# Nineteen TensorE steps of a list-scheduled kernel get later places, with what depends on them

## The chip, the cores and the metric

The kernel runs on one core of a Trainium2 chip. That core has five engines with queues of their own: TensorE (PE), VectorE (DVE), ScalarE (ACT), GpSimd (POOL) and SyncE (SP), which mostly issues transfers. The metric is the time of one execution on the device in microseconds (us), as the median of several runs.

## The reference

One layer of a streaming encoder: `x` is 1024 tokens by 1024 features, float32.

```python
mod = silu(c) @ ada_w + ada_b                      # six vectors of 1024: shift, scale, gate, twice
h = modulate(rms_norm(x, mix_norm_w), sh_m, sc_m)
proj = h @ w_in                                    # one input projection for both head groups
y_r = rwkv7_group(proj[..., :RWKV_COLS], ...)      # 8 heads x 64
y_m = mlstm_group(proj[..., RWKV_COLS:], ...)      # 4 heads, qk 64, v 128
x = x + gate * (concat(y_r, y_m) @ w_out)
x = x + gate * hier_moe(modulate(rms_norm(x, ffn_norm_w), sh_f, sc_f), ...)   # 32 experts, 2 per token
out = rms_norm(x, final_norm_w)
```

The RWKV-7 group carries one 64x64 state per head over the tokens:

```python
def step(state, inp):
    r_t, w_t, k_t, v_t, kk_t, b_t = inp
    sa = einsum('bhij,bhj->bhi', state, -kk_t)
    state = state * w_t[:, :, None, :] + sa[..., None] * b_t[:, :, None, :] + v_t[..., None] * k_t[:, :, None, :]
    return state, einsum('bhij,bhj->bhi', state, r_t)
```

The mLSTM group does the same with a matrix memory, gates and a running maximum, in chunks of 64 tokens.

## The kernel before, in words

The kernel computes the RWKV recurrence in chunks of 64 tokens. Eight units are worked off (four pairs of heads, two halves of the sequence), each with eight chunks. A unit has stages, and each is a generator that yields between pieces of work. `unit_prep` makes `AR`, `BK`, `kk`, `Ei` and the products `tp<-AR,BK`, masked by VectorE into `G`. `unit_solve` inverts the triangular matrices that couple tokens within a chunk: it stores `G`, loads it as `N16` (`N` in the profile), and VectorE runs fifteen pairs of `Xt<-N,XD` (a product) and `XD<-Xt` (a sum). The result goes to memory as `img` and comes back as two tiles, `D16` first and then `X16` (`D` and `X` in the profile, issued by SyncE one after the other). `unit_levels` builds larger blocks of the inverse: `tp<-D,G`, VectorE's `T`, `tp<-T,X`, VectorE's `D`, and two more levels. `unit_scan` goes through the chunks: `pr<-st,AR`, VectorE's `R`, `pu<-R,X`, VectorE's copies `UV`, `pp<-UV,BKT`, VectorE's new state `st`, and `py` with the output. `unit_post` normalizes it to `Y`.

Beside the units run the input projection (`lane` steps: three matmuls, since each operand is split into a high and a low part: `hTh,whi`, `hTl,whi`, `hTh,wlo`), the modulation vectors (`ada_w` is multiplied into `ada_rest` on VectorE; TensorE then sums over partitions with `tp<-ones,ada_rest`, and VectorE copies the sums to `modc`), the gates of the mLSTM (`lg`, `row_lf`, `row_m`), its chunks, and transposes of `x` (`lxs`, `lxt`, stored as `xTd`).

The order of this mixer stage is planned. `Recorder.add` doesn't issue an instruction, it records an operation with its dependences; matmuls in a row into the same output tile become one operation, called a step here. `Recorder.flush` then runs a list scheduler over all recorded operations of the five engines, with a cost for each from `Recorder.cost`, ranks by kind of work, and limits by the buffers of each pool. It gives each operation a beginning in planned time (`o.begin`) and appends it to `self.plan`. In the end it issues them in this order:

```python
        for o in self.plan:
            o.run()
```

Each engine executes its own instructions in the order of issue. What an instruction must wait for on other engines, and for a buffer's earlier users, is found when it is issued; so an engine waits at the head of its queue, whatever stands behind. All recorded operations carry line 262 in the profile, the call in `add`. TensorE's steps are numbered in the order of the plan, from 0; there are 1064 of them. The recorded stage takes TensorE from 63.8 to some 800 us of the span. Before it lie the first normalization and modulation, behind it the output projection, the routing and the experts; these are not reordered.

Of the kernel before, what the change touches and what calls it, by code (L numbers as in the profile page):

```python
# [192 lines left out]
PRIO = dict(prep=2, rest=3, lev=1, scan=0, post=4, gates=6, ada=9, rx=8, h=3, chunk=5, split=5, prod=7, fin=4, fetch=5, y=4)  # L193
PE_SLACK = 0.5
RANK = 20.0


class Recorder:
# [55 lines left out]
    def add(self, engine, what, a, kw):  # L254
# [53 lines left out]
        if o.pe:  # L308
            self.last = o

    def flush(self):

        ops = self.ops
# [11 lines left out]
        for o in ops:  # L325
            o.rank = RANK * o.rank - o.bl
        order = {}
# [44 lines left out]
        while left:  # L372
            busy = False
            for e in free:
# [9 lines left out]
                o = best  # L384
# [29 lines left out]
            assert nxt, ('stuck', now, left, [(e, [(o.what, o.seq, [t.key[1] for t in o.tiles]) for o in c[:6]]) for e, c in cand.items()])  # L414
            now = min(nxt)
        self.mode = 'direct'
        for o in self.plan:
            o.run()
        self.ops, self.history, self.last, self.last_pool = [], {}, None, None
# [2130 lines left out]
```

## Time and profile before

| | |
|---|---|
| median of 3 runs | 1297.64 us (1297.11, 1297.64, 1306.84) |
| the profiled execution | 1305.22 us, span 1303.3 us |
| mean granted clock of TensorE | 0.91 of full speed |
| TensorE (PE) busy | 1148.8 us, 88% of the span |
| VectorE (DVE) | 936.3 us, 72% |
| ScalarE (ACT) | 529.2 us, 41% |
| GpSimd (POOL) | 393.9 us, 30% |

The shares are means over stages with different limits, so the trace is read by stretch and by place. A row of the timeline gives the start and the duration in us, the engine, the line, the operation with its output and inputs, and behind it, in brackets, how long the engine was idle before it and what released it. [...]

### The profile page before, as it was taken

The numbers are of one execution on the slowest core, as the hardware profiler recorded it, in microseconds if no ns is written. First come the engines' busy times: TensorE is split into PE (matmuls) and PEld (weight loads), VectorE is DVE, ScalarE is ACT, GpSimd is POOL, SyncE is SP. The second block draws the span as 40 slices with busy tenths as digits, with TensorE's granted clock in tenths as the row PEclk, the third lists the DMA queues.
The fourth block names the chain that finished last, engine by engine and source line by source line (L and its number), as shares of the span: only waits on it lengthen the run. The fifth ranks groups of instructions, "written<-read, shape, count | busy, mean of one in ns | idle before, by whom it ended". The sixth has DMA issues, their size and how long they took to land.

```text
span 1303.3 us, 21771 instructions
## 1 busy us (share of the span) xinstructions
PE 1148.8 (88%) x7807; PEld 836.3 (64%) x7807; DVE 936.3 (72%) x2024; ACT 529.2 (41%) x1021; POOL 393.9 (30%) x464
## 2 busy tenths in 40 slices
PE   3886889797999999999898899995899999898893
PEld 3665666676676777776666677774666666565553
DVE  6699676876656878877748554834688888777766
ACT  5343112142433443333422333644455655455444
POOL 4623134221233242432133323543222222222112
PEclk8887677698999999999899699997799999999997
DMA  9525555475433443322433554699599999999974
GB/s 313 153 69 155 180 174 153 122 204 158 136 96 97 107 112 80 104 69 61 94 119 102 154 159 134 195 361 326 190 306 314 302 289 285 282 320 326 324 264 164
DMA packets 251935, 246.16 MB, mean 189 GB/s; under 512 B 55064, under 2 KB 190362, under 8 KB 251824
## 3 DMA queue, kind: packets, MB, share of 16 engines
q1 hardware_dynamic: 243504, 228.43, 56.2%
q0 software_dynamic: 8320, 16.31, 5.4%
q8 instruction: 62, 1.02, 0.3%
q14 instruction: 49, 0.40, 0.1%
HBM read 212.13 MB, written 44.74 MB: 197 GB/s over the span
## 4 chain that ended last, share of the span: by engine, by line
PE 62%; DMA 16%; DVE 13%; issue 3%; ACT 2%; SPq 1%; POOL 1%; DVEq 0%; ACTq 0%; POOLq 0%
PE lane L262 20%; PE tp L262 14%; PE yd L2049 8%; DMA wd<-in_moe_w_down_dram 4%; PE lane L787 4%; PE lane L788 4%; PE lane L789 3%; DMA ada_w<-in_ada_w_dram 2%; DMA D<-img 2%; DMA wa<-in_moe_w_gate_dram 2%; PE tp L2002 2%; PE lane L189 2%; PE py L262 1%; DMA X<-img 1%; DVE Xt L262 1%
## 5 line engine op out<-in xcount | busy, mean ns | idle before, releaser
L262 PE MATMUL lane<-hTh,whi 128*128 128x512 f32 (+1 forms) x469 | 213.5, 455 | 2.5 <-DVE v L262 0.7
L262 PE MATMUL lane<-hTl,whi 128*128 128x512 f32 (+1 forms) x469 | 192.3, 410 | 5.7 <-DVE hTl L262 5.7
L262 PE MATMUL lane<-hTh,wlo 128*128 128x512 f32 (+1 forms) x469 | 190.8, 407 | 3.1 <-DVE wlo L262 3.1
L262 ACT CAST whi<-wraw 128x512 fp32r<-128x512 f32 (+1 forms) x120 | 71.6, 607 | 163.8 <-PE lane L262 133.8
L2049 PE MATMUL yd<-wd,a 128*112 128x512 f32 x256 | 119.8, 607 | 12.5 <-DMA wd<-in_moe_w_down_dram 9.3
L262 POOL TENSOR_TENSOR wlo<-wraw,whi 128x512 fp32r<-128x512 f32 (+1 forms) x60 | 81.9, 1367 | 97.2 <-ACT whi L262 95.1
L262 PEld LDWEIGHTS lane<-hTh,whi 128*128 128x128 f32 (+1 forms) x469 | 91.0, 194 | 30.9 <-issue 2.2
L262 PEld LDWEIGHTS lane<-hTh,wlo 128*128 128x128 f32 (+1 forms) x469 | 90.9, 194 | 27.2 <-DVE wlo L262 4.8
L262 PEld LDWEIGHTS lane<-hTl,whi 128*128 128x128 f32 (+1 forms) x469 | 91.4, 195 | 20.6 <-DVE hTl L262 8.3
L1972 DVE TENSOR_TENSOR wl<-wa,wh 128x1024 fp32r<-128x1024 f32 x62 | 75.6, 1225 | 40.2 <-ACT wh L1971 38.8
L787 PE MATMUL lane<-wh,xh 128*112 128x512 f32 x256 | 103.9, 406 | 0.0
L788 PE MATMUL lane<-wl,xh 128*112 128x512 f32 x256 | 101.7, 397 | 0.0
L789 PE MATMUL lane<-wh,xl 128*112 128x512 f32 x256 | 100.7, 393 | 0.0
L262 POOL TENSOR_SCALAR sW<-st,WT 128x64 f32<-128x64 f32 x56 | 33.1, 592 | 215.5 <-DVE st L262 129.9
L2076 POOL DMA_INDIRECT x2d<-ys,idx x30 | 44.9, 1496 | 147.4 <-DVE ys L2060 138.5
L2049 PEld LDWEIGHTS yd<-wd,a 128*112 128x112 f32 x256 | 43.5, 182 | 65.4 <-issue 44.6
L1972 DVE TENSOR_TENSOR wl<-wb,wh 128x1024 fp32r<-128x1024 f32 x62 | 76.4, 1233 | 11.3 <-ACT wh L1971 9.6
L1971 ACT CAST wh<-wa 128x1024 fp32r<-128x1024 f32 x62 | 64.8, 1049 | 45.4 <-PE lane L789 36.5
L1971 ACT CAST wh<-wb 128x1024 fp32r<-128x1024 f32 x63 | 66.2, 1051 | 17.4 <-PE lane L789 8.3
L1978 POOL DMA_INDIRECT xt<-xad,idx x32 | 35.0, 1093 | 113.3 <-PE tp L2002 94.9
L262 DVE COPY UV<-pu 64x64 f32<-64x64 f32 x128 | 28.1, 220 | 38.3 <-PE pu L262 36.9
L789 PEld LDWEIGHTS lane<-wh,xl 128*112 128x112 f32 x256 | 44.9, 175 | 14.8 <-DVE xl L2015 0.4
(515 smaller groups left out, 2539.2 us busy)
## 6 DMA issues: line engine op xcount, KB each, us to landing
wd<-in_moe_w_down_dram SPq DMA_DIRECT2D x64, 512.0 KB
wraw<-in_w_in_dram SPq DMA_DIRECT2D x104, 256.0 KB
ada_w<-in_ada_w_dram SPq DMA_DIRECT2D x32, 512.0 KB
wa<-in_moe_w_gate_dram SPq DMA_DIRECT2D x32, 512.0 KB
wa<-in_moe_w_up_dram SPq DMA_DIRECT2D x32, 512.0 KB
wb<-in_moe_w_gate_dram SPq DMA_DIRECT2D x32, 512.0 KB
wb<-in_moe_w_up_dram SPq DMA_DIRECT2D x32, 512.0 KB
ada_w<-in_ada_w_dram SPq DMA_DIRECT2D x32, 256.0 KB
```

The costliest lines, as they stand in the source:

```text
L189: return getattr(eng, what)(*[real(x) for x in a], **{k: real(x) for k, x in kw.items()})
L262: call = lambda: getattr(fn, what)(*[real(x) for x in a], **{k: real(x) for k, x in kw.items()})
L787: nc.tensor.matmul(ps, l[0], r[0], start=first, stop=False)
L788: nc.tensor.matmul(ps, l[0], r[1], start=False, stop=False)
L789: self.mark = nc.tensor.matmul(ps, l[1], r[0], start=False, stop=last)
L1971: nc.scalar.copy(h, src)
L1972: (engs[n] if engs else nc.vector).tensor_tensor(l, src, h.bitcast(F32), op=ALU.subtract)
L1978: return self.nc.gpsimd.indirect_dma_start(out=self.xts[e % 3], out_offset=None, in_=self.xad[:], in_offset=bass.IndirectOffsetOnAxis(ap=s ...
L2002: self.nc.tensor.transpose(pt[:, j, :], v[:, j // 2, j % 2], self.ident[0:SL, 0:SL])
L2049: self.nc.tensor.matmul(y[:, b], a[:, i], d[:, i, b * 512:b * 512 + 512], start=(i == 0), stop=(i == 1))
L2076: self.nc.gpsimd.indirect_dma_start(out=self.x2d[:], out_offset=bass.IndirectOffsetOnAxis(ap=oi, axis=0), in_=ys, in_offset=None, bounds_c ...
```

## The change

A table gives, for nineteen of TensorE's steps, a number of microseconds. A new function `put_off` runs once, between the planning and the issue. It keeps each operation's planned beginning as its key; a step in the table gets its beginning plus the table's number, and whatever depends on it, or takes over a buffer that a postponed operation used before, gets at least the same key. Then the plan is sorted by key; ties keep their order. No operation is added, removed or changed.

```diff
+LATE = {4: 3.4, 44: 2.1, 64: 4.7, 66: 4.9, 73: 3.7, 103: 2.6, 105: 1.5, 107: 1.0, 142: 1.8, 188: 2.1, 196: 3.5, 273: 5.8, 276: 0.9, 358: 0.9, 670: 1.7, 798: 4.5, 911: 1.6, 912: 4.0, 943: 3.0}
...
+    def put_off(self):
+
+        pos = {o: i for i, o in enumerate(self.plan)}
+        old = {}
+        for ts in self.slots.values():
+            for a, b in zip(ts, ts[ts[0].bufs:]):
+                if b.ops_of:
+                    old.setdefault(min(b.ops_of, key=pos.get), []).extend(a.ops_of)
+        key, no = {}, 0
+        for o in self.plan:
+            key[o] = max([o.begin] + [key[d] for d in o.deps if key[d] > d.begin] + [key[d] for d in old.get(o, ()) if d is not o and key[d] > d.begin])
+            if o.pe:
+                key[o] = max(key[o], o.begin + LATE.get(no, 0.0))
+                no += 1
+        self.plan.sort(key=lambda o: (key[o], pos[o]))
+
...
         self.mode = 'direct'
+        self.put_off()
         for o in self.plan:
             o.run()
```

The numbers in the table are the idle times that the trace of the kernel before has ahead of these steps, rounded; they add up to 53.7 us. The order changes at 64 places of TensorE's queue, 45 of VectorE's and 8 of ScalarE's; GpSimd and SyncE keep theirs. The steps, by place (letters are used below):

| place | step | what it is | now behind |
|---|---|---|---|
| A | 4 | `py<-st,AR` | 5 (`lane`), 6 (`tp<-ident,nrm`), 7 (`lane`) |
| B | 44 | twelve gate transposes `lg`, `row_lf`, `row_m` | 45, 46 (`lane`) |
| C | 64 | `tp<-ident,BK` | 65 (the same) |
| D | 66 | `tp<-AR,BK` | 67, 68, 70, 71 |
| E | 73 | `tp<-ones,ada_rest` | 74 (`tp<-D,G`), 75 (`lane`) |
| F | 103, 105, 107 | `pp<-UV,BKT`, `pr<-st,AR`, `tp<-headsel,sq` | 104; 106; none |
| G | 142 | `tp<-D,G` with D16 | 143 (`tp<-ones,ada_rest`) |
| H | 188, 196 | `tp<-ones,ada_rest`, `tp<-ident,lxs` | 189, 190 (`pp`, `py`); 197, 198, 199, 201 |
| I | 273, 276 | `tp<-D,G` with D16, `tp<-AR,BK` | 274, 275, 277, 278; 277, 278 |
| J | 358 | `tp<-D,G` with D16 | 359 (`py`), 360 (`lane`) |
| K | 670 | `tp<-D,G` with D16 | 671 (`pu`), 672 (`lane`), 673 (`tp<-ident,mnv`) |
| L | 798 | `tp<-D,G` with D16 | 799 (`lane`), 800 (gate transposes), 803 (`lane`) |
| M | 911, 912 | `tp<-ident,Y`, `tp<-ident,mnv` | 913 (`tp<-mqo`); 913, 914, 916 |
| N | 943 | `tp<-D,G` with D16 | 944 (`tp<-ident,ex`), 945 to 948 (`lane`) |

At place E, on VectorE's queue, the row sums' copy to `modc` stood ahead of `carry` and `u`, which VectorE takes out of the `lane` step. Before:

```order
L262 SCALAR_TENSOR_TENSOR qko<-lane,phalf,qko 128x510
L262 COPY modc<-tp 128x8
L262 SCALAR_TENSOR_TENSOR qko<-lane,phalf,qko 128x509
L262 TENSOR_SCALAR carry<-lane,pcol 128x1
L262 COPY u_257<-lane 128x3
L262 SCALAR_TENSOR_TENSOR qko<-qks,qko 128x512
L262 TENSOR_TENSOR Xt<-N_1383,XD 64x1
```

and with the change:

```order
L263 SCALAR_TENSOR_TENSOR qko<-lane,phalf,qko 128x510
L263 SCALAR_TENSOR_TENSOR qko<-lane,phalf,qko 128x509
L263 TENSOR_SCALAR carry<-lane,pcol 128x1
L263 COPY u_257<-lane 128x3
L263 COPY modc<-tp 128x8
L263 SCALAR_TENSOR_TENSOR qko<-qks,qko 128x512
L263 TENSOR_TENSOR Xt<-N_1374,XD 64x1
```

`modc` moved behind `u`; the last `qko` product and the first `Xt` of a solve stand directly behind it.

At place F, on VectorE's queue, is the state update `st` of a scan (the numbers behind `N` name buffers). Before:

```order
L262 TENSOR_TENSOR Xt<-N_1383,XD 64x11x11
L262 SCALAR_TENSOR_TENSOR st<-pp,WT,sW 128x64
L262 TENSOR_REDUCE XD<-Xt 64x11
L262 SCALAR_TENSOR_TENSOR k<-lane,pcol,k 128x511
L262 TENSOR_TENSOR Xt<-N_1383,XD 64x12x12
L262 SCALAR_TENSOR_TENSOR cs<-cmask,sw 128x512
```

and with the change:

```order
L263 TENSOR_TENSOR Xt<-N_1374,XD 64x11x11
L263 TENSOR_REDUCE XD<-Xt 64x11
L263 SCALAR_TENSOR_TENSOR k<-lane,pcol,k 128x511
L263 TENSOR_TENSOR Xt<-N_1374,XD 64x12x12
L263 SCALAR_TENSOR_TENSOR cs<-cmask,sw 128x512
L263 SCALAR_TENSOR_TENSOR st<-pp,WT,sW 128x64
```

`st` moved behind four instructions, the scan `cs` among them.

At place L, on TensorE's queue, 798 is the group of 32x32 products with `D_6794` (alternating with two buffers of `G`). Before:

```order
L262 MATMUL tp<-D_6794,G_6398 32x32 x2
L262 MATMUL lane<-hTh,whi 128x512
L262 MATMUL lane<-hTl,whi 128x512
L262 MATMUL lane<-hTh,wlo 128x512
L262 MATMUL tp<-ident,lg_6610 128x4 x4
L262 MATMUL tp<-ident,row_lf 128x4 x4
L262 MATMUL tp<-ident,row_m 128x4 x4
L262 MATMUL tp<-T_6872,X_6802 32x32 x32
L262 MATMUL tp<-ident,vcm 128x128 x4
```

and with the change:

```order
L263 MATMUL tp<-ident,lg_6610 128x4 x4
L263 MATMUL tp<-ident,row_lf 128x4 x4
L263 MATMUL tp<-ident,row_m 128x4 x4
L263 MATMUL lane<-hTh,whi 128x512
L263 MATMUL lane<-hTl,whi 128x512
L263 MATMUL lane<-hTh,wlo 128x512
L263 MATMUL tp<-D_6794,G_6379 32x32 x2
...
L263 MATMUL tp<-T_6921,X_6802 32x32 x32
L263 MATMUL tp<-ident,vcm 128x128 x4
```

One `lane` step (799) now stands ahead of the gate transposes and another (803) behind them, and the D group follows, directly ahead of `tp<-T,X` (801). On VectorE, `T` moved behind three operations on `Y` and a `wlo`.

## Rows read from the trace of the kernel before

**Rows 1.** Two stretches: us, engines' busy us (instructions), PEclk, DMA share, GB/s

```profile
64.00:160.00 96.00, 75.58 (x599) 56.72 (x598) 81.68 (x160) 31.58 (x57) 23.96 (x26) 0.79 0.47 132
800.00:1303.00 503.00, 445.03 (x1982) 309.65 (x1980) 368.78 (x548) 255.89 (x446) 140.88 (x130) 0.94 0.85 278
```

**Rows 2.** Waits of TensorE, 64 to 800 us: total us, times, longest

```profile
PE tp L262 <- DMA D<-img: 17.6, 6, 5.8
```

**Rows 3.** Timeline at place B: start, us, engine, operation, [idle before, releaser]

```profile
105.83 0.76 PE L262 MATMUL lane<-hTh,whi 128*128 128x512 f32 x1 [0.17 <-DVE carry L262]
```

**Rows 4.** Timeline at place E, TensorE

```profile
143.10 3.54 PE L262 MATMUL tp<-ones,ada_rest 128*128 128x1 f32 x16 [3.73 <-issue]
...
149.26 0.96 PE L262 MATMUL tp<-X,T 32*32 32x32 f32 x28
```

**Rows 5.** Timeline at place E, VectorE

```profile
146.68 0.17 DVE L262 COPY modc<-tp 128x8 f32<-128x8 f32 x1 [0.71 <-PE tp L262]
...
147.42 0.21 DVE L262 TENSOR_SCALAR carry<-lane,pcol 128x1 f32<-128x1 f32 x1
...
149.73 0.15 DVE L262 TENSOR_TENSOR Xt<-N,XD 64x1 f32<-64x1 f32 x1
```

**Rows 6.** Timeline at place F, VectorE and TensorE

```profile
170.53 0.28 DVE L262 SCALAR_TENSOR_TENSOR st<-pp,WT,sW 128x64 f32<-128x64 f32 x1
...
171.89 1.21 DVE L262 TENSOR_TENSOR_SCAN cs<-cmask,sw 128x512 f32<-128x512 f32 x1
...
172.52 1.87 PE L262 MATMUL tp<-headsel,sq 128*128 128x2 f32 x8 [0.95 <-ACT sq L262]
...
175.04 2.29 PE L262 MATMUL tp<-ones,ada_rest 128*128 128x1 f32 x10 [0.24 <-DVE ada_rest L262]
```

**Rows 7.** Chain of waits at place G: start, us, what

```profile
196.59 9.07 DMA X<-img
```

**Rows 8.** Timeline at place H, TensorE

```profile
236.66 3.57 PE L262 MATMUL tp<-ones,ada_rest 128*128 128x1 f32 x16 [2.14 <-DVE ada_rest L262]
...
248.26 1.12 PE L262 MATMUL tp<-ident,lxs 128*128 128x128 f32 x4 [3.46 <-DMA lxs<-in_x_dram]
```

**Rows 9.** Timeline at place H, VectorE

```profile
237.99 0.23 DVE L262 COPY UV<-pu 64x64 f32<-64x64 f32 x1
```

**Rows 10.** Timeline at place I, TensorE

```profile
310.77 0.75 PE L262 MATMUL tp<-T,X 32*32 32x32 f32 x64
```

**Rows 11.** Timeline at place I, ScalarE

```profile
305.36 0.58 ACT L262 COPY lxt<-tp 128x512 f32<-128x512 f32 x1 [8.31 <-DMA xTd<-lxt]
```

**Rows 12.** Timeline at place L, TensorE

```profile
636.89 1.08 PE L262 MATMUL tp<-D,G 32*32 32x32 f32 x64 [4.46 <-DMA D<-img]
...
640.84 1.08 PE L262 MATMUL tp<-T,X 32*32 32x32 f32 x64
...
644.04 0.63 PE L262 MATMUL lane<-hTh,whi 128*128 128x512 f32 x1
```

**Rows 13.** Issue of X at place L, and what transfers moved, 636 to 640 us in 40 slices

```profile
631.66 0.52 SPq L262 DMA_DIRECT2D X<-img  x1
...
GB/s 31 21 20 31 51 41 51 51 41 51 51 41 61 41 51 51 41 51 51 41 51 51 41 61 41 51 51 41 41 72 21 20 31 21 0 0 0 0 0 0
```

**Rows 14.** Timeline at place N, TensorE and SyncE

```profile
748.53 0.51 SPq L262 DMA_DIRECT2D X<-img  x1
...
754.49 1.08 PE L262 MATMUL tp<-D,G 32*32 32x32 f32 x64 [2.95 <-DMA D<-img]
...
759.77 0.75 PE L262 MATMUL tp<-T,X 32*32 32x32 f32 x64
```

**Rows 15.** Timeline at place M, TensorE

```profile
714.89 1.81 PE L262 MATMUL tp<-ident,mnv 128*128 128x128 f32 x4 [4.03 <-DVE Xt L262]
```

**Rows 16.** Three stretches of the recorded stage, columns as in rows 1

```profile
634.70:644.80 10.10, 7.91 (x152) 6.63 (x153) 5.14 (x10) 3.44 (x7) 3.76 (x4) 0.50 0.27 68
775.00:781.00 6.00, 6.00 (x50) 4.76 (x48) 4.83 (x18) 2.93 (x11) 1.75 (x2) 1.00 0.70 210
781.20:784.80 3.60, 3.60 (x12) 2.38 (x12) 1.10 (x5) 0.00 (x0) 1.84 (x2) 0.53 0.14 41
```

## The prediction

> **What bounds the kernel now.** Start with busy time by stretch. From 64 to 160 us TensorE works 75.58 of 96 us and VectorE 81.68: there the two hand work to each other, and neither is free. From 800 us on it works 445 of 503 us with the DMA engines 85% busy [rows 1]. The changed table holds only places between those marks, so next comes the list of what TensorE waited for in that stretch: the longest entry is the landing of `D<-img`, 17.6 us in six waits [rows 2]. The table's values are the traced waits before its nineteen steps and add up to 53.7 us. That is what the change could win if each wait were filled with other work and if nothing else waited. So the third view is the timeline around each step: what stands behind the moved step, and what does that wait for? I read every place that way, with the plan's dependences beside the times. Engines obey their queues in order, so a moved step moves its readers too.
>
> The profiled execution took 1305.22 us; its span is 1303.3. The median of three runs is 1297.64, 7.6 us less. I make the sum against 1305.22 and apply it to the median.
>
> **Places that come out at nothing.** 64 and 65 change places, and wait for the same `BK`; 103 and 104 for the same `UV`; 105 and 106 for the same `st`; 66 goes behind 67 and 68, which want the same GpSimd `AR`; 107 passes nothing. 4 goes behind three steps that VectorE releases late, before a stretch where VectorE sets the pace. 358 (J) waits for D, and the steps let past it only come nearer to the wait for X, which ended the place before as well. I take 0 for each; a gain of J's 0.9 us or a loss of 0.4 us at step 4 are the bounds.
>
> **Early places that lose.**
> B, step 44: twelve gate transposes began at 104.22 after a wait of 2.1 us. Behind 45 they must wait until VectorE has written `carry`, which let 45 start at 105.83 even so [rows 3]; the idle time grows to about 3.6 us, and their 1.4 us come on top. Part of that hides under VectorE, which is busy back to back here. I take **+0.9**, bounds 0 and 1.4.
> E, step 73, the row sums of `ada_rest`: 3.54 us at 143.10 [rows 4]. In the new order 74 runs at 143.4 to 144.4. Then 75 waits for `carry`, which ends at 147.63 now and near 146.9 with `modc` out of its way [rows 5]; it ends at 148.5, 73 at 151.9, and step 76 starts there and not at 149.26 [rows 4]: **+2.6**. Below it is 0 (VectorE sets the pace anyway), above +4.3 (3.54 whole, and 0.75 us more). VectorE's `modc` now stands behind `u`, so it holds `qko` and the first `Xt` of the triangular solve until 73 is done: 152.2 for 149.73 [rows 5].
> F, steps 103, 105, 107: on VectorE the state update `st` falls behind `k`, `Xt` and the scan `cs`, which ends at 173.10 [rows 6]. `st` is done at 173.4 instead of 170.81. 105 follows it; the 1.87 us of 107 and the 0.5 us of 108 must still run before 109, which started at 175.04 after 0.24 us of waiting. That gives 176.0, **+0.95**, bounds 0 and 2.5.
> G, step 142, gives a part back. Step 145 waits for X, which landed at 196.59 + 9.07 = 205.66 [rows 7], in either order. The 1.8 us spent on D before it are now filled, so up to 1.8 us of E and F vanish there, if X lands no later; but the solve that feeds X moved too. I take half, **-0.9**, bounds 0 and -1.8.
> H, steps 188 and 196: 188 is 3.57 us long [rows 8]. 189 goes first and waits for `UV`, written at 237.99 + 0.23 [rows 9]; 188 then ends near 242.7, where it ended at 240.23: +2.0 on 191, with what 190 fills. At 196 the wait for `lxs` (3.46 us, rows 8) is filled with 197, but 198 and 199 wait for VectorE's next `UV` and `BK`, so only 0.6 comes back. **+1.4**, bounds 0 and 2.6.
> I, steps 273 and 276, the largest wait (5.8 us). 274, 275 and 277 fill from 296.4 on. 278 then needs ScalarE's `lxt`, which starts at 305.36 after 8.31 us of waiting for the store `xTd` [rows 11], and 273 needs the copy behind it. 280 comes at 311.0 for 310.77 [rows 10]. **+0.2**, bounds -3.5 (if `lxt` didn't hold 278) and +0.7.
>
> **Late places that gain.**
> L, step 798: 4.46 us of waiting [rows 12]. 799 runs at once, 800 waits for ScalarE's `row_m`, 803 for its `vcm`, and by the durations of their rows 803 ends near 637.3 and 798 at 638.2. Then 801 waits for X. Issued at 631.66, its bytes flow until 639.4, the 34th of 40 slices of 636 to 640 [rows 13]; with the last write I take 639.56. 801 started at 640.84 and 804 at 644.04; now 804 starts near 641.3: **-2.7**, bounds -4.5 and -2.3.
> N, step 943: 2.95 us [rows 14]. Five ready steps fill it. 949 started at 759.77. X was issued at 748.53 [rows 14]; with the flight of L's X (7.7 us, rows 13) and of G's (9.07, rows 7) it lands between 756.2 and 757.6. Starting at 757.24 would be -2.5. The solved steps then run before the clock is back, so I take **-1.7**, bounds -0.8 and -3.0.
> K, step 670: a wait of 1.7 us, and X comes soon after; **-0.5**, bounds 0 and -1.7.
> M, steps 911 and 912: 913 fills 1.2 us, 912's 4.03 us [rows 15] can't be filled, since the steps let past want VectorE's `kw` of the same moment. That is -0.9 at step 918, but N's wait for X is anchored on the solve and takes it back: **0**, bounds 0 and -1.5.
>
> **The sum**: 0.9 + 2.6 + 0.95 - 0.9 + 1.4 + 0.2 = +5.15; -2.7 - 1.7 - 0.5 = -4.9; together **+0.25**. The stages behind 800 us keep their order and start when this one lets them, so the shift is carried. 1297.64 + 0.25 is 1298. With every term at its low bound (J's -0.9 among them): -16.9, or 1281; with every one at its high bound (step 4's +0.4 too): +8.8, or 1306.
>
> **The clock.** A granted clock of 0.50 (1.2 GHz) stood over 634.7 to 644.8, right behind L's wait. But from 775 to 781 TensorE worked 6.00 of 6.00 us at 1.00, and from 781.2 to 784.8 it had 0.53 without a wait [rows 16]. So a filled gap doesn't assure the clock, and I count nothing for it; if it did, the work of L from 641.3 to 644.8 would run in half the time, 1.8 us less. [...]
>
> **Rivals.**
> 1. Waits are filled, and the clock comes back: every term at its low bound, and 1.8 us of L's slow stretch besides, -18.7: 1279. For it: 14.8 of the 53.7 us lie in K to N, where much ready work stands behind. Against: whatever fills, the wait for X stands close behind D. [...] Chance 0.10.
> 2. On the other side: VectorE's queue becomes the bound. `modc` behind 73 holds the solve and the `qko` products, `st` behind `cs` holds the scan, and nothing gives it back at G. E +4.3, F +2.5, H +2.6, B +1.4 and the rest at their high bounds: +8.8, 1306. It decides once E, F and H together exceed the 4.9 us of the late gains. For it: 152.2 for 149.73 in the solve. Against: X at G landed after 9.07 us in a crowded queue, so the solve had slack there. Chance 0.17.
> 3. The change does almost nothing it says: a step and the one that takes its place wait for the same thing, or the step passes nothing, as at five places above. Every term 0: 1297.6. For it: those five. Against: 73 and 798 pass steps that wait for other things. Chance 0.10.
>
> **The numbers.** The forecast has 0.63, at **1298**, its own range 1292 to 1304 (late gains and early losses each wrong by half). The range goes to 1286 below, leaving out most of rival 1, and to 1306 above, rival 2 at full price; about 0.18 is outside. One per cent, 13 us, is what a measurement can tell, as three runs of the kernel before spread over 9.7 us. Faster than that needs rival 1: 0.10. Slower needs rival 2 and more: 0.05. Within: 0.85.
>
> **What would show it.** In the new profile: the idle time on TensorE before `ones,ada_rest` near 144 is there still, before the `lane` group; `modc` starts after 151; `st` comes after `cs` near 173; before `T,X` the releaser is `X<-img` near 205.7, 639.6 and 757.2, where `D<-img` was before; step 804 is near 641 plus what the early places lost. Wrong would be waits for D that vanish with no wait for X behind them, a `modc` that doesn't delay `Xt`, or a different clock over whole stretches, which could outweigh every term here.

## The result and the profile after

The kernel with the change takes 1320.19 us (median of four runs, 1310.44 to 1322.44) beside 1297.38 for the kernel before. The ratio is **1.0121** (95% interval 1.0078 to 1.0164), and 1.0103 (1.0069 to 1.0137) when it was measured a second time beside other runs of the kernel before. The two medians alone would give 1.018; over twelve runs of the change and 123 of the kernel before, the means differ by 14.9 us, or 1.1%. In ratios and means, runs more than 1.5% above the fastest of their kernel are left out (of the kernel before nine of 132, up to 1318.6 us). The change is some 14 us slower and lies outside the range of 1286 to 1306. The forecast, no change, did not hold.

Where the time went is read from two stretches: the recorded stage, from its first TensorE step to its last, and what stands behind it. (The last step ends at 835.45 us, so what lies directly behind 800 us still belongs to the stage.) Columns are as in rows 1. The kernel before:

```profile
63.79:835.45 771.66, 698.19 (x5865) 521.35 (x5866) 550.02 (x1444) 260.02 (x582) 234.64 (x294) 0.90 0.45 125
...
835.45:1303.30 467.85, 412.21 (x1781) 283.64 (x1780) 342.70 (x485) 238.49 (x392) 125.04 (x115) 0.94 0.88 289
```

and with the change:

```profile
63.48:852.47 788.99, 714.14 (x5865) 533.77 (x5866) 554.36 (x1448) 261.28 (x583) 236.67 (x296) 0.88 0.44 122
...
852.47:1320.40 467.93, 413.15 (x1782) 284.41 (x1780) 341.85 (x481) 237.85 (x390) 122.06 (x113) 0.93 0.88 288
```

The stages behind take the same time, 467.85 and 467.93. The recorded stage is 17.33 us longer, and hardly any of this is waiting: the same 5865 matmul records keep TensorE busy for 714.14 us where it was 698.19, 15.95 more, at a granted clock of 0.88 for 0.90. The idle time is 788.99 - 714.14 = 74.85 us, and was 73.47. So the nineteen waits were neither filled nor made worse as a whole; **the same work ran slower**. Weighted with the clock granted at each moment, the busy time comes to 634.7 us at full speed before and to 634.6 with the change, so all of the 15.95 us is the clock: the stage spends 194.6 us at a granted clock of 0.50 where it spent 160.4. (Where the texts on record write 1.2 GHz, they mean a granted clock of 0.50: the profile gives a share of full speed, and no run shows a frequency.) A second profiled execution of the change says the same:

```profile
63.60:850.98 787.38, 712.00 (x5865) 532.30 (x5866) 552.86 (x1444) 260.29 (x582) 234.73 (x294) 0.88 0.44 122
```

It is 15.72 us longer than before, 13.81 of it work (635.4 us at full speed).

What TensorE waits for has changed, as this list for 64 to 812 us shows (total us, times, longest):

```profile
PE lane L263 <- DVE carry L263: 6.2, 2, 3.8
PE pp L263 <- DVE UV L263: 5.6, 2, 3.6
PE tp L263 <- DVE BK L263: 5.6, 3, 4.6
PE tp L263 <- POOL AR L263: 4.9, 1, 4.9
...
PE tp L263 <- DMA X<-img: 3.7, 3, 1.8
```

`D<-img`, 17.6 us before [rows 2], is gone from the head of it (0.3 us are left). The steps that were let past now wait themselves: 45 and 75 for `carry`, 189 and 198 for `UV`, 65 and 67 for what 64 and 66 waited for.

At place E, TensorE's timeline and VectorE's, to be read beside rows 4 and 5:

```profile
151.30 0.80 PE L263 MATMUL lane<-hTh,whi 128*128 128x512 f32 x1 [2.48 <-DVE carry L263]
...
152.75 3.41 PE L263 MATMUL tp<-ones,ada_rest 128*128 128x1 f32 x16
156.09 1.06 PE L263 MATMUL tp<-X,T 32*32 32x32 f32 x32
```

```profile
156.19 0.17 DVE L263 COPY modc<-tp 128x8 f32<-128x8 f32 x1 [4.88 <-PE tp L263]
...
156.88 0.14 DVE L263 TENSOR_TENSOR Xt<-N,XD 64x1 f32<-64x1 f32 x1
```

VectorE stands 4.88 us at `modc`, with the solve's first `Xt` behind it. This is the chain that the prediction wrote down, at later times, because the places ahead had lost time already. Place F, VectorE and then TensorE, beside rows 6:

```profile
179.71 1.21 DVE L263 TENSOR_TENSOR_SCAN cs<-cmask,sw 128x512 f32<-128x512 f32 x1
180.84 0.25 DVE L263 SCALAR_TENSOR_TENSOR st<-pp,WT,sW 128x64 f32<-128x64 f32 x1
```

```profile
181.14 0.37 PE L263 MATMUL py<-st,AR 64*64 64x64 f32 x2 [3.70 <-DVE st L263]
```

Before, TensorE had two shorter waits here:

```profile
168.86 0.34 PE L262 MATMUL pp<-UV,BKT 128*64 128x64 f32 x4 [2.64 <-DVE UV L262]
...
170.87 0.37 PE L262 MATMUL pr<-st,AR 64*64 64x64 f32 x2 [1.45 <-DVE st L262]
```

With the change `st` follows `cs`, and the waits of 2.64 and 1.45 us became one of 1.36 and one of 3.70.

Place H shows the part that was missed. The stretch runs from the end of step 187 to the end of step 215. Before:

```profile
234.51:264.00 29.49, 23.17 (x152) 18.26 (x151) 23.34 (x57) 5.87 (x10) 5.78 (x6) 0.65 0.36 101
```

With the change, and below it the piece of it in which TensorE never waits:

```profile
243.06:279.16 36.10, 29.36 (x150) 23.23 (x151) 23.16 (x57) 5.87 (x10) 5.86 (x6) 0.53 0.35 97
...
260.09:278.80 18.71, 18.71 (x84) 15.39 (x84) 9.11 (x20) 4.56 (x8) 0.45 (x1) 0.50 0.31 94
```

The idle time is 6.74 us for 6.32. All the rest of the 6.6 us is work at the lower clock: TensorE is busy for 18.71 of 18.71 us, and the clock stays at 0.50 for all of them. In the kernel before it came back at 255.8, in step 202, where with the change it came back only at 278.8, in step 214. The pieces on either side read:

```profile
251.31:255.80 4.49, 4.49 (x26) 4.02 (x26) 2.25 (x5) 0.69 (x1) 0.45 (x1) 0.50 0.18 65
255.80:264.00 8.20, 7.89 (x69) 6.34 (x68) 5.49 (x13) 3.97 (x7) 0.00 (x0) 1.00 0.31 86
```

Of the late places, L gained and N gave its gain back. L, beside rows 12:

```profile
654.08 1.00 PE L263 MATMUL tp<-D,G 32*32 32x32 f32 x64
656.64 1.08 PE L263 MATMUL tp<-T,X 32*32 32x32 f32 x64 [1.56 <-DVE T L263]
...
658.41 0.78 PE L263 MATMUL lane<-hTh,whi 128*128 128x512 f32 x1
```

The wait for D is gone, and a shorter one for VectorE's `T` (the profile's attribution) stands behind it. N, beside rows 14, and a stretch of it:

```profile
769.13 0.75 PE L263 MATMUL tp<-D,G 32*32 32x32 f32 x64
770.85 0.74 PE L263 MATMUL tp<-T,X 32*32 32x32 f32 x64 [0.97 <-DMA X<-img]
```

```profile
773.70:787.40 13.70, 13.70 (x103) 10.88 (x103) 1.62 (x6) 5.79 (x26) 2.01 (x2) 0.50 0.43 122
```

949 starts after 0.97 us on X instead of 2.95 on D, and three microseconds later the clock falls for 13.70 us without a wait. In this execution that takes back all that the place had won (steps 941 to 985 take 35.4 us, 34.2 before); in the second one they take 30.8.

### The profile page after: what moved, and what is told of

Same layout as the page of the kernel before. It is cut to its first block, busy times and chain, and to the rows that moved or that the text cites. A ratio compares the mean times of both kernels' runs of the same rounds, so it can differ in the third digit from the quotient of the medians.

```text
span 1320.4 us, 21772 instructions
## 1 busy us (share of the span) xinstructions
PE 1164.4 (88%) x7807; PEld 848.1 (64%) x7807; DVE 940.1 (71%) x2024; ACT 529.6 (40%) x1021; POOL 393.1 (30%) x464
## 4 chain that ended last, share of the span: by engine, by line
PE 65%; DMA 14%; DVE 13%; issue 3%; ACT 2%; SPq 1%; POOL 1%; DVEq 0%; ACTq 0%; POOLq 0%
PE lane L263 22%; PE tp L263 15%; PE yd L2067 7%; DMA wd<-in_moe_w_down_dram 3%; PE lane L805 3%; PE lane L806 3%; PE lane L807 3%; PE lane L189 3%; DMA wa<-in_moe_w_gate_dram 2%; DMA X<-img 2%; PE py L263 2%; PE tp L2020 2%; DMA ada_w<-in_ada_w_dram 1%; PE tp L189 1%; PE pu L263 1%
## 5 line engine op out<-in xcount | busy, mean ns | idle before, releaser
L263 PEld LDWEIGHTS lane<-hTl,whi 128*128 128x128 f32 (+1 forms) x469 | 92.4, 197 | 21.1 <-DVE hTl L263 8.3
L263 POOL TENSOR_SCALAR sW<-st,WT 128x64 f32<-128x64 f32 x56 | 33.4, 597 | 231.3 <-DVE st L263 149.2
L1989 ACT CAST wh<-wa 128x1024 fp32r<-128x1024 f32 x62 | 65.0, 1051 | 45.8 <-PE lane L807 35.5
L263 DVE TENSOR_TENSOR wlo<-wraw,whi 128x512 fp32r<-128x512 f32 (+1 forms) x60 | 52.2, 871 | 4.4 <-ACT whi L263 4.1
```

The source lines that it names most:

```text
L263: call = lambda: getattr(fn, what)(*[real(x) for x in a], **{k: real(x) for k, x in kw.items()})
L1989: nc.scalar.copy(h, src)
```

## The experiments

Two theories were set against each other: that waiting explains the loss (VectorE's queue held by `modc` and `st`, the wait moved from one step to another), and that the clock does (TensorE runs the same steps longer at a granted clock of 0.50). A third is chance, since the time of one and the same kernel varies (1296.04 to 1306.84 us in four runs of the kernel before). A kernel that puts off only some steps has a shorter table, for instance

```diff
-LATE = {4: 3.4, 44: 2.1, ..., 943: 3.0}
+LATE = {670: 1.7, 798: 4.5, 911: 1.6, 912: 4.0, 943: 3.0}
```

**Halves.** The late five, then the early fourteen:

> Only steps 670, 798, 911, 912 and 943 are put off; the other fourteen keep their places. Waiting theory (what counts is who waits for what): the idle time removed at 798 and 943, 2.3 and 2.0 us in the trace of the change, is gained: 1293 us for 1297.4. Clock theory (the waits stay nearly the same in sum, and the change loses because the same steps run longer at 1.2 GHz): 798 gains its 2 us, 943 pays 3 to 4.5 us back at the lower clock as it did in the full change: 1296 to 1299. Chance theory (the clock differs between executions and has nothing to do with the order): anywhere in 1293 to 1306.

> Only the fourteen steps from 4 to 358 are put off. Waiting theory: +5 us by the prediction's terms, 1302. Clock theory: all of the loss is here, +15 to +19 us, 1312 to 1317, with the mean granted clock at 0.90 and TensorE's idle time in the recorded stage within 2 us of before. Chance theory: 1296 to 1307.

Measured: 1.0003 (0.997 to 1.0035) and 1.0105 (1.0072 to 1.0138). The whole loss is in the early places, as the clock theory had it; the late ones come to nothing, where the prediction had -4.9 us. The early fourteen have a median of 1318.27 us and a mean clock of 0.901, as the change has. Their profiled execution, though, is one of their fastest, 1308.61 us, and doesn't show this loss. Its recorded stage and place H:

```profile
63.10:838.77 775.67, 699.57 (x5865) 522.79 (x5866) 547.72 (x1442) 260.42 (x582) 235.57 (x294) 0.90 0.45 124
238.25:274.03 35.78, 28.92 (x150) 23.08 (x151) 23.23 (x57) 5.87 (x10) 5.76 (x6) 0.52 0.35 98
```

With the stage's clock at 0.90, as in the kernel before, it is 4.0 us longer, 2.6 of it idle time. That is near the +5.15 that the prediction had for the early places. H is slow here too, but steps 905 to 925 and 941 to 985 took 10.5 us less than before (from 320 to 860 us the granted clock was 0.97, and 0.95 in the kernel before).

**Work in the waits.** TensorE gets throwaway matmuls ahead of steps that wait, first with nothing put off, then with the whole change. They write the tile that the step overwrites (the code is shortened):

```diff
+FILL = {44: 2, 64: 5, 66: 5, 73: 4, 103: 3, ..., 798: 8, 911: 2, 912: 6, 943: 5}
...
         for o in self.plan:
+            if o.pe and o.fill:
+                t = ...  # the output tile of the step, first 256 columns
+                for _ in range(o.fill):
+                    self.nc.tensor.matmul(t[:, 0:n], ident, cmask[:, 0:n], start=True, stop=True)
             o.run()
```

> Nothing is put off. Ahead of eighteen of the nineteen steps (not 4, whose output tile holds other sums already) TensorE gets throwaway matmuls of 128x256 float32 into the step's own output tile, which the step then overwrites: some 60 to 80% of the traced wait. No wait is removed, none is moved. Waiting theory: no change, or up to 5 us slower where they outlast the wait: 1297 to 1303. Clock theory: TensorE has no long pause, the stretches at 1.2 GHz shrink from 160 us in the recorded stage, and 10 to 30 us are gained: 1267 to 1287, with a mean clock above 0.93. Chance theory: 1296 to 1307.

> The whole change, all nineteen steps put off, and throwaway matmuls as in the run before ahead of the nineteen steps that now wait longest. Waiting theory: as slow as the change, 1318 to 1323. Clock theory: the loss goes away and more: 1270 to 1295, mean clock above 0.93. Chance theory: 1310 to 1322.

The first: **0.9944** (0.9913 to 0.9975), a median of 1295.46 us for 1301.62. That is faster, though by 6 us where 10 to 30 were expected; the mean clock is 0.931, where the kernel before had 0.912 beside it, and 113 us of the recorded stage are at 0.50. Waiting alone can't explain that a kernel gets faster by useless work. The second: 1.0132 (1.0091 to 1.0174), no better than the change, though the clock of its profiled execution was 0.920. That speaks against the clock theory only at first sight. The trace shows that seven of its nineteen groups didn't run during the wait but behind it: the tile they write is still being read by the very instruction that is waited for. They added 17.8 us (4.07 at 108, 4.02 at 734, 2.86 at 324 and four shorter ones). So this run decides nothing.

The same with wide bfloat16 matmuls, to see whether the kind of work counts (shortened as well):

```diff
-                    self.nc.tensor.matmul(t[:, 0:n], ident, cmask[:, 0:n], start=True, stop=True)
+                    self.nc.tensor.matmul(t[:, 0:n], busy, busy.unsqueeze(1).to_broadcast([P, n // P, P]), ...)   # bfloat16, n up to 512
```

> Nothing is put off. The throwaway matmuls are now bfloat16, 512 columns each (fewer where the tile is smaller), in the same eighteen waits. If what TensorE does decides the clock (wide one-pass matmuls lift it, float32 transposes and small products do not, whether there is a pause or not), they hold it better than the float32 ones did: under 90 us at 1.2 GHz in the recorded stage (113 with float32, 160 before) and 1280 to 1291 us, ratio 0.985 to 0.992. If only pauses count, the kind makes no difference: ratio 0.994 as with float32. If the clock has nothing to do with it: 1.000.

> The whole change with the same wide matmuls ahead of nineteen steps that wait in it. Kind-of-work theory: the stretch at 1.2 GHz around 245 to 279 us, which float32 dummies did not shorten, breaks up, steps 188 to 215 take 30 to 33 us (36.1 with the change, 38.3 with float32 dummies), and the time falls to 1293 to 1305. Pause theory: as with float32 dummies, 1.013. Waiting theory (VectorE's queue): 1.012.

Measured: 0.9955 (0.9918 to 0.9993), no better than float32, and with 113 us at 0.50 in the recorded stage, as with float32, where under 90 were expected; so this idea is not borne out. And 1.0162 (1.0102 to 1.0222), again with groups that run behind the wait, as these rows of place H show:

```profile
246.44 3.51 PE L444 MATMUL pp<-busy 128*128 128x64 bf16 x72 [3.75 <-DVE UV L264]
...
260.51 1.86 PE L444 MATMUL pp<-busy 128*128 128x64 bf16 x32 [1.96 <-DVE UV L264]
```

**Place H in parts.**

> Only step 196 (four transposes of lxs) is put off, behind 197, 198, 199 and 201. By the prediction's term it gains 0.6 us. By the trace of the change it costs: the two 512-column steps 197 and 200 are driven apart by a wait, and the clock stays low through the products and transposes behind them: steps 188 to 215 take 33.5 to 35 us for 29.5, the run is 3 to 5 us slower (ratio 1.003 to 1.004).

> Only step 188 (row sums of ada_rest) is put off, behind 189 and 190. By the prediction +2.0 us, by waiting alone: steps 188 to 215 take 31.5 us. By the clock theory no more than that, since 197 and 200 stay together: ratio 1.001 to 1.002. If 188 is what keeps the clock low, 34 to 36 us.

Measured: 1.0011 (0.997 to 1.0052), with steps 188 to 215 at 33.4 us; and 1.0056 (1.0023 to 1.0089), with 36.4 us. With 188 put off, 1.9 us of H's loss is idle time and 5.0 us is work; with 196 put off, the idle time is 1.1 us less and the work 5.0 more. Almost the whole of H with 196 put off, 30.70 us of it, ran at a granted clock of 0.50:

```profile
234.60:265.30 30.70, 26.50 (x136) 20.31 (x136) 20.71 (x54) 5.87 (x10) 3.41 (x5) 0.50 0.41 114
```

These two profiles don't show that the moved step lowers the clock. In the seven profiled executions in which H takes 29 us, the clock had come up 16.2 to 16.8 us ahead of the end of step 187. In these two it had come up 18.0 and 18.1 us ahead of it, although nothing that early is moved in either kernel. With the fourteen early steps put off it came up 16.3 us ahead and fell 0.7 us behind step 187, as in five of the seven, and yet came back only 34.9 us behind it: there the difference does begin in H.

**Single places.** The eight-step set keeps only fills that ran during their wait.

> Nothing is put off; float32 throwaway matmuls (128x256) only ahead of the eight steps where the first such run gained by the step table: 142, 188, 196, 273, 358, 670, 798, 943. Clock theory: it keeps the gains (2 us each at 142, 188 to 196, 273 and 670, 3 at 798 and 943) and loses what they cost ahead of 44, 103 and 911: ratio 0.989 to 0.994, so faster than both kernels. Waiting theory: 1.000, since no wait is shorter.

> Only step 73 (row sums of ada_rest) is put off, behind 74 and 75. By the prediction's term: steps 61 to 86 take 2.6 us more than the 38.9 of before, modc starts after 151 and the first Xt of the solve near 152.2, and the run is that much slower at the same clock (ratio 1.002). Clock theory: the same in waits, and more only where the clock in steps 61 to 110 differs: 1.002 to 1.004.

> Only step 44 (twelve gate transposes) is put off, behind 45 and 46. By the prediction's term +0.9 us in steps 44 to 60; with the change it was +3.0, with the fourteen early steps +1.0. If the wait sets it: +1.0 to +1.5 (idle time 3.75 for 2.30, and no more). If the clock does: up to +3, of which the idle time explains 1.45. Ratio 1.000 to 1.003.

> The change once more, unaltered, for its spread. Over 46 runs of the kernel before, time and mean granted clock go together (correlation -0.85, 7.8 us per 0.01). Clock theory: the change's runs fall on a line with the same slope, their mean clock is 0.90 to 0.903 for 0.911, and half of its loss or more is the difference in clock. Chance theory: with more runs its mean clock comes to 0.91 and the ratio falls to 1.005 or less. Waiting theory: the clock is the same as before in the mean and the ratio stays at 1.012.

The eight fills: **0.9934** (0.990 to 0.9967), 1295.98 us beside 1304.20, faster than both kernels, with a mean clock of 0.922. Its recorded stage and its place H:

```profile
63.98:828.42 764.44, 706.42 (x5933) 526.84 (x5934) 551.21 (x1448) 261.29 (x583) 235.77 (x296) 0.91 0.46 126
236.84:263.24 26.40, 23.57 (x165) 18.32 (x165) 23.12 (x57) 5.87 (x10) 5.86 (x6) 0.81 0.40 112
```

and place L of it:

```profile
628.66 3.62 PE L444 MATMUL tp<-cmask,ident 128*128 128x256 f32 x16
633.67 0.75 PE L264 MATMUL tp<-D,G 32*32 32x32 f32 x64 [1.40 <-DMA D<-img]
```

The step waits for the same D, but TensorE was at work until 1.40 us ahead of it, and its 64 matmuls take 0.75 us at a granted clock of 1.00 (633.67 to 640 us), where they took 1.08 at 0.50 before [rows 12, 16]. H takes 26.40 us for 29.49 although some 5.5 us of its work is useless. In the whole stage 18.6 of the 706.42 us are throwaway matmuls, so the kernel's own steps take 688 us where they took 698.

Step 73 alone: 1.0013 (0.9977 to 1.0048). Steps 61 to 86 take 41.4 us for 38.9, so its term of +2.6 is right to 0.1; `modc` starts at 150.64 and `Xt` at 151.32, both a little earlier than expected. H is slower in this profile, yet the stage as a whole is busy for 699.12 us, 0.9 more than before: the work of other places took that much less. Step 44 alone: 0.9957 (0.993 to 0.9984), *faster*, though its place loses 2.8 us in the profiled execution, which with 1309.56 us is one of its longer ones (median 1300.18). A loss at a place doesn't say what the run does. The gain itself may be chance: of some nineteen 95% intervals, one is expected to miss. And in both of these kernels place H, where nothing is moved, is slower. 73 alone, then 44 alone:

```profile
235.61:269.32 33.71, 27.55 (x151) 22.45 (x151) 23.29 (x57) 5.87 (x10) 5.75 (x6) 0.54 0.38 105
```

```profile
237.74:271.47 33.73, 27.42 (x151) 22.57 (x151) 23.35 (x57) 5.87 (x10) 5.77 (x6) 0.60 0.38 104
```

The idle time is 6.2 and 6.3 us, as before; the work takes 4.3 us more, at a granted clock of 0.54 and 0.60 for 0.65. A wait can't do this. In both, the clock had come up 17.9 and 18.1 us ahead of the end of step 187, as with 188 or 196 alone; whether 73 and 44 did that isn't shown. That H comes later in the span isn't the reason: with 798, with 103 to 107 or with 4, 64 and 66 put off it begins at 238.0 to 238.7 us, behind both of these, and takes 28.9 to 29.5 us.

The change once more: 1.0103. Over its twelve runs the mean clock is 0.9012 and the mean time 1317.7; over 123 runs of the kernel before 0.9113 and 1302.8. So neither chance (a mean clock near 0.91, a ratio of 1.005 or less) nor waiting alone (the same clock as before) fits. Among these 123, time and clock go together (correlation -0.79), 7.2 us for 0.01. By that line 7.3 of the 14.9 us go with the clock. The line is an average: it counts stretches at 0.50 in which TensorE waits anyway (33.5 of the 160.4 us in the recorded stage before, 35.5 of 194.6 with the change), while in the profiled execution the work alone explains 15.95 of 17.33. What the other half of the loss is in the runs that weren't profiled isn't shown.

**What was left.**

> Only steps 103, 105 and 107 are put off, so that VectorE's st falls behind the scan cs. Prediction's term: +0.95 us, st after 173 and step 110 one us later: ratio 1.001 at the same clock. If the rest of the early loss is here: 1.003. Clock theory: the sign may be hidden by a change of mean clock of 0.002, 1.6 us either way.

> Only steps 273 and 276 are put off. Prediction's term: +0.2 us, since lxt holds 278: ratio 1.000. If place I is where the missing 4 us are: 1.003. Steps 269 to 290 took 23 to 32 us over the profiles so far, by the clock they met.

> Only step 798 is put off, behind 799, 800 and 803. Prediction's term: -2.7 us; with the change steps 791 to 812 took 1.4 to 1.9 us less. Ratio 0.998 to 0.9985 if a gain at a place reaches the end. 1.000 if the later wait for X at step 949 or the expert stage behind takes it back.

> Only step 943 is put off, behind 944 to 948. Prediction's term: -1.7 us, ratio 0.9987. If what it gains is paid back because the clock falls behind it (with the change steps 941 to 985 took 30.8 and 35.4 us in two profiles, 34.2 before): 1.000.

> Only steps 4, 64 and 66 are put off. Prediction's terms: 0, at most +0.4: ratio 1.000. If they hold the part of the early loss that is not found: +3 to +4 us, 1.003, most of it in steps 61 to 86, because 66 now stands ahead of 69 and 72 and delays T,X and the levels behind it.

> The throwaway matmuls of the eight-step run, and step 44 put off as in its own run. If the two gains add up (7.8 and 3.2 us in the means): 1292, ratio 0.991 to 0.992. If the gain of 44 alone was a luckier clock and nothing of the order: as with the eight-step run, 0.993 to 0.995.

| kernel | ratio, 95% interval | own place, us (before) |
|---|---|---|
| 103, 105, 107 | 0.9991, 0.9963 to 1.0019 | 87 to 110: 22.1 (21.1) |
| 273, 276 | 1.0026, 0.9998 to 1.0053 | 269 to 290: 31.6 (25.1) |
| 798 | 0.9978, 0.9944 to 1.0012 | 791 to 812: 21.6 (23.7) |
| 943 | 0.9978, 0.9942 to 1.0015 | 941 to 985: 33.0 (34.2) |
| 4, 64, 66 | 1.0006, 0.9973 to 1.0039 | 61 to 86: 39.1 (38.9) |
| eight fills and 44 | 0.9952, 0.9923 to 0.9982 | 44 to 60: 20.0 (17.0) |

The terms of F (+0.95, measured 1.0) and of steps 4, 64 and 66 (nothing) hold. Place I takes 31.6 us with 273 and 276 put off, but 29.9 to 31.0 in three other executions in which nothing in it is moved, with the idle time within 0.8 us of before in all four: its loss is the same work running longer, which it did unmoved as well. 798 and 943 each look like the predicted gain, though neither is clear of no change, and both together with their neighbours give 1.0003. The fills and step 44 don't add up, so nothing confirms the gain of 44 alone. The ratios of the seven early kernels (44, 73, 188, 196, and three of this table) sum to +0.6%; the fourteen steps together give +1.05%. Two of the fourteen, 142 and 358, were not put off alone, and the uncertainty of a sum of seven such ratios, some 0.9%, is larger than the difference, so these numbers don't show that the parts work on each other.

## Why the prediction was wrong

**The step that failed** is "So a filled gap doesn't assure the clock, and I count nothing for it". The rows behind it were right, but they show that the clock can move either way (1.00 and 0.53 in two stretches in which TensorE never waits), and the prediction took that as a term of zero. In the two profiled executions this term is +15.95 us of the 17.33 in the stage and +13.81 of 15.72, more than the upper bounds of all waits together (+8.8). It should have been an unknown with bounds of its own: the recorded stage ran at 0.90 before and at 0.88 with the change, and the same work of H took 23.17 us and 29.36. The prediction did name "a different clock over whole stretches, which could outweigh every term here" among its signs of being wrong, but gave it neither a term nor a chance.

**The waits** came out well in sum: the prediction said +0.25 us, and the stage's idle time went up by 1.38. That is in part luck. E: +2.6, measured 2.5 alone. F: +0.95, measured 1.0. But L, -2.7, measured -1.9 with the change and -2.1 alone, outside its bounds: 1.56 us of waiting are left there, for which the profile names VectorE's `T`. And G, -0.9, has 1.7 us more idle time in steps 142 to 160. H's wait at 188: +2.0, and step 191 came 1.8 us later. M was taken as zero at the end and gained 0.5 (steps 905 to 925). The releaser before 949 is X, as said; before 145 and 801 the profile names VectorE instead.

**The terms that were mis-sized** are those whose work met the low clock for longer: B had 10.2 us at 0.50 for 6.8 before, H 34.1 for 20.5, I 13.7 for 10.2, N 13.7 for 6.8. B, +0.9, was +3.0: 1.45 of it idle time, over its upper bound already, since VectorE didn't hide it, and 1.57 work. H, +1.4, was +6.6: 0.42 idle, 6.19 work. I, +0.2, was +1.8 (idle time 0.7 less, work 2.5 more). N, -1.7, was +1.2: idle 2.0 less, work 3.2 more. The work in these differs from execution to execution: in the second one of the change I is +6.4 and N -3.4, while B (+2.9) and H (+5.9) stay.

**The rivals.** The second came nearest, 1306 at most, but by another mechanism. VectorE's queue did what it describes, and cost about what the forecast gave it (E 2.5, F 1.0). The first was wrong about the change, whose stage ran at 0.88 for 0.90, and right about the kernel: the eight fills in the waits gained about 0.7%, with a mean clock of 0.922 beside 0.911, but the moved steps did not (0.901). The third fits steps 4, 64 and 66 (1.0006 alone), not E or H.

**Still open.** Why the clock comes back 21 us behind step 187 when none of 44, 73, 188 and 196 is put off, and 33 us behind it with 73, 44 or 196 put off, is not settled. Whether the size of a pause, the kind of the kernel's own work or the moment decides can't be told from these runs. The kind of the throwaway work made no difference with nothing put off; with the change that test was spoiled, since part of its work came behind the waits. That the change is slower as a whole because of the clock is shown in two profiled executions and by the run means; how much of the 1.1% is clock in every execution is not.

## What to carry to other kernels

When an order of work is changed, split the difference of a stretch into idle time and time of the same instructions; here a list of waits explained 1.4 of 17 us, and the granted clock the rest. A wait that is moved to the next step is no gain (the idle time was 74.85 us here, and 73.47 before), and steps that nobody moved can run several microseconds slower in another execution (4.3 us of work at H with 73 or 44 alone), so one profile of a kernel doesn't show what a moved step did to the clock. Where TensorE must wait, throwaway matmuls into the waiting step's own tile gained about 0.6% here; they must not go where the tile's last reader is the thing that the step waits for (seven such groups ran behind their waits and added 17.8 us).

## What the runs showed that was not expected

The 123 runs of the unaltered kernel lie between 1292.7 and 1311.5 us, and much of the spread goes with the mean clock (correlation -0.79). Place H takes 28.9 to 29.5 us in seven profiled executions without fills in which none of 44, 73, 188 and 196 is put off, and 33.4 to 38.5 in nine in which one of them is (two of these with fills); a tenth, with 44 put off and fills, took 27.5. In the four of the nine with one step alone the clock came up at another moment already ahead of H (17.9 to 18.1 us ahead of the end of step 187, where it was 16.2 to 16.8 in the seven). With the change the clock stayed at 0.50 through 18.7 us in which TensorE never waited, and fell to it for 13.7 us behind a wait of 0.97 us; so neither its fall nor its return could be read off the waits beside it.
